# Reciprocal square roots of all norms: a chain of eleven VectorE instructions replaced by one GpSimd power instruction

## The chip, the cores and the metric

The kernel runs on one core of a Trainium2 chip. The core has TensorE for matrix products and transposes (PE in the profile, with its weight loads as PEld), VectorE (DVE), ScalarE (ACT), GpSimd (POOL) and SyncE, which issues most DMAs here (SP, its queue SPq). They run their own streams of instructions and meet through semaphores. The metric is the device time of one launch in microseconds, as a median of several runs.

## The reference, cut to what matters

One encoder layer is applied to two requests of 2048 tokens with 1024 features, in fp32. The normed input goes through one projection whose columns are split among two branches of attention. Both norm their queries and keys per head of 64 values:

```python
def rms_norm(x, g):
    y = xf * lax.rsqrt(jnp.mean(xf * xf, axis=-1, keepdims=True) + EPS)
    return (y * g).astype(x.dtype)

h = rms_norm(x, norm_w)
q_a, k_a, v_a, g_a, q_b, k_b, v_b, g_b = jnp.split(h @ w_in, IN_SPLITS, axis=-1)
q_a = partial_rope(rms_norm(q_a, q_norm_a), pos)    # 8 heads
k_a = partial_rope(rms_norm(k_a, k_norm_a), pos)    # 2 heads
o_a = windowed_gqa_sink(q_a, k_a, v_a, sink_a) * silu(g_a)
q_b, k_b = rms_norm(q_b, q_norm_b), rms_norm(k_b, k_norm_b)
o_b = neighbourhood_attn(q_b, k_b, v_b, rpb_b) * silu(g_b)
x = x + concat(o_a, o_b) @ w_out
x = x + (p @ w_ple) * sigmoid(x @ w_ple_gate)
```

Every `rsqrt` is one value per token (the norm of the input) or one per token and head (the norms of queries and keys).

## The kernel before, in words

Matrix products with full fp32 accuracy are made of three products of rounded halves: each operand is split into a rounded high part (written by ACT) and the rest (by DVE or POOL).

The program has three stages. In the **windowed stage**, 16 blocks of 128 tokens for each of two requests, about 57 to 770 us, each step of the loop projects one block (`proj_a`, L376) while PE also does the attention of the block before (`unit_a`, L492, two key-value heads, hence two units for each block). In the **neighbourhood stage**, about 772 to 1842 us, 64 steps do the same with `proj_b` (L559) and `unit_b` (L629): two halves of the heads, each over both requests. The **last stage** makes the output projection, the gate and the residual; it has no norms.

The input is not normed before it is projected. The projections are taken of the raw input and the factor is put in afterwards. So a block's norms need the mean square of the token (`square`, L283, by ACT from tiles `stn` that SP loads) and the mean squares of the projected heads, and then a reciprocal square root of each: `rsqrt` (L118). It is called

- in the key half of `proj_a` (L391): `vr` 8:11, three columns, two key heads and the token itself. Of its result `y` come the normed keys `kt` (L394, DVE), the values `vv` (L397, ACT) and the scale of the gate.
- in the query half of `proj_a` (L425): eight columns. Of them comes `q` (L427, DVE), which POOL then rotates (`rope`, L405 to L408).
- in `proj_b` (L584): eight columns, four key heads and four query heads. Of them come `kb` and `qg` (L588, DVE).
- in `stats_b` (L481): sixteen columns, twice in the program.

`rsqrt` takes a first guess from the bits of the number (L121, L123), then three Newton steps of three instructions each (L126, L127, L128), eleven DVE instructions on tiles of 128 partitions and 3, 8 or 16 columns.

The attention unit makes four score tiles (`sc`, `scb`: matmul L189), which DVE adds a mask or bias to and reduces to a maximum (L204); after the fourth, DVE negates the maxima (L215, L217), ACT takes four exponentials (L219) and PE transposes them (`pt`, `ptb`, L192). The score tiles and the transposes share three PSUM buffers, so that the fourth score tile is written where the first one was.

The order of PE is written out: `pinned` (L180) chains every matmul and transpose to the one before it, after a table of positions that mixes attention with the projections. The order of the other engines is the scheduler's, which takes each engine's instructions by when it estimates that they can run; it may move them past each other unless they depend on one another. Each engine then runs its own stream strictly in that order. At the end of each request, `regroup` (L469) writes the tokens' mean squares to memory and reads them back in another arrangement with 16 small loads on SP.

POOL makes the lower halves of the input (`xr`, L279), the rotations and the products with the gate (`g`, L229).

Of the kernel before, what the change touches and what calls it, by code (L numbers as in the profile page):

```python
# [11 lines left out]
F32 = mybir.dt.float32  # L12
F32R = mybir.dt.float32r
I32 = mybir.dt.int32
AF = mybir.ActivationFunctionType
ALU = mybir.AluOpType
# [4 lines left out]
NT = SEQ // 128  # L21
# [63 lines left out]
def emit(ctx, tc, io):  # L85
    nc = tc.nc
    dram = ctx.enter_context(tc.tile_pool(name="dram", bufs=1, space=bass.MemoryType.DRAM))
    cp = ctx.enter_context(tc.tile_pool(name="const", bufs=1))
# [11 lines left out]
    rs_b = cp.tile([128, 2 * NT], F32, tag="rs_b", name="rs_b")  # L100
    hr_b = cp.tile([128, 2 * NT], F32, tag="hr_b", name="hr_b")
    ep_b = cp.tile([128, 2 * NT], F32, tag="ep_b", name="ep_b")
    ms_b = cp.tile([128, 2 * NT], F32, tag="ms_b", name="ms_b")
    wk = cp.tile([128, 2], F32, tag="wk", name="wk")
    wkt = cp.tile([128, 4], F32, tag="wkt", name="wkt")
    nc.sync.dma_start(wkt, io["qk_norms"])
# [8 lines left out]
    ob_d = [dram.tile([4, 128, 4, 4, 128], F32, tag=f"ob_d{s}", name=f"ob_d{s}") for s in range(2)]  # L115
    ms_d = dram.tile([2 * SEQ], F32, tag="ms_d", name="ms_d")

    def rsqrt(pool, v, y, n, tag):  # L118
        i2 = pool.tile([128, n], I32, tag=tag + "i", name=tag + "i")
        a = pool.tile([128, n], F32, tag=tag + "a", name=tag + "a")  # L120
        nc.vector.tensor_scalar(out=i2, in0=v.bitcast(I32), scalar1=1, scalar2=None,  # L121
                                op0=ALU.logical_shift_right)
        nc.vector.tensor_scalar(out=y.bitcast(I32), in0=i2, scalar1=-1, scalar2=0x5F3759DF,  # L123
                                op0=ALU.mult, op1=ALU.add)
        for _ in range(3):
            nc.vector.scalar_tensor_tensor(out=a, in0=y, scalar=-0.5, in1=y, op0=ALU.mult, op1=ALU.mult)  # L126
            nc.vector.tensor_tensor(out=a, in0=a, in1=v, op=ALU.mult)  # L127
            nc.vector.scalar_tensor_tensor(out=y, in0=a, scalar=1.5, in1=y, op0=ALU.add, op1=ALU.mult)  # L128

    copies = []  # L130

# [113 lines left out]
    ap = ab_stack.enter_context(tc.tile_pool(name="ab", bufs=1))  # L245
# [98 lines left out]
    for i in range(4):  # L344
        nc.vector.tensor_tensor(out=tab[i // 2][:, i % 2], in0=cs[:, i % 2],
                                in1=rw[:, i].unsqueeze(1).broadcast_to([128, NT, 16]), op=ALU.mult)
# [29 lines left out]
    def proj_a(f):  # L376
# [8 lines left out]
                                op=ALU.add, axis=AX.X)  # L385
        vr = ap.tile([128, 11], F32, tag="vr", name="vr", bufs=2)
        y = ap.tile([128, 12], F32, tag="y", name="y", bufs=4)
        nc.vector.tensor_scalar(out=vr[:, 8:10], in0=ssq[:, 8:10], scalar1=1.0 / HD, scalar2=ee,
                                op0=ALU.mult, op1=ALU.add)
        nc.vector.tensor_scalar(out=vr[:, 10:11], in0=ms, scalar1=EPS, scalar2=None, op0=ALU.add)  # L390
        rsqrt(ap, vr[:, 8:11], y[:, 8:11], 3, "rqk")  # L391
        nc.vector.tensor_scalar_mul(y[:, 11:12], y[:, 10:11], 0.5)
        kt = ap.tile([128, 4, HD], F32, tag="kt", name="kt", bufs=2)
        nc.vector.tensor_tensor(out=kt[:, 0:2, :], in0=pk[:, 0:128].rearrange("p (h d) -> p h d", d=HD),  # L394
                                in1=y[:, 8:10].unsqueeze(2).broadcast_to([128, 2, HD]), op=ALU.mult)
# [3 lines left out]
                                       in1=vv[:, t, :, 0, :].bitcast(F32), op0=ALU.mult, op1=ALU.subtract)  # L399
# [12 lines left out]
        for i, c in enumerate(project(pq, xr, lambda k, b: w_q[k][:, b, :], 215)):  # L412
# [5 lines left out]
            if i == ka:  # L418
# [3 lines left out]
        nc.vector.tensor_reduce(out=ssq[:, 0:8], in_=sq.rearrange("p (h d) -> p h d", d=HD), op=ALU.add, axis=AX.X)  # L422
        nc.vector.tensor_scalar(out=vr[:, 0:8], in0=ssq[:, 0:8], scalar1=1.0 / HD, scalar2=ee,
                                op0=ALU.mult, op1=ALU.add)
        rsqrt(ap, vr[:, 0:8], y[:, 0:8], 8, "rqa")  # L425
        q = ap.tile([128, 8, HD], F32, tag="qg", name="q", bufs=6)
        nc.vector.tensor_tensor(out=q, in0=pq.rearrange("p (h d) -> p h d", d=HD),  # L427
                                in1=y[:, 0:8].unsqueeze(2).broadcast_to([128, 8, HD]), op=ALU.mult)
# [15 lines left out]
        if f == NT + 4:  # L444
            stats_b(0)
# [30 lines left out]
    def stats_b(s):  # L476
        c = slice(NT * s, NT * s + NT)
        tc.keep_in_program_order(nc.vector.tensor_scalar(out=ep_b[:, c], in0=ms_b[:, c], scalar1=EPS,
                                                         scalar2=EPS * EPS, op0=ALU.mult, op1=ALU.add))
        nc.vector.tensor_scalar(out=ms_b[:, c], in0=ms_b[:, c], scalar1=EPS, scalar2=None, op0=ALU.add)  # L480
        rsqrt(ap, ms_b[:, c], rs_b[:, c], NT, "rsb")  # L481
        nc.vector.tensor_scalar_mul(hr_b[:, c], rs_b[:, c], 0.5)

    def prep_a(f):
# [74 lines left out]
    def proj_b(f):  # L559
# [3 lines left out]
        if f == 2 * NT + 4:  # L563
            stats_b(1)
# [6 lines left out]
        for i, c in enumerate(project(pk, xr, lambda k, b: w_qk[k][:, b, :], 215)):  # L571
            at = i + 24 if f in last else i
            if at in HX:
# [6 lines left out]
        vr = ap.tile([128, 8], F32, tag="vr", name="vrb", bufs=2)  # L580
        y = ap.tile([128, 8], F32, tag="y", name="yb", bufs=4)
        nc.vector.tensor_scalar(out=vr, in0=ssq, scalar1=1.0 / HD, scalar2=ep_b[:, st:st + 1],
                                op0=ALU.mult, op1=ALU.add)
        rsqrt(ap, vr, y, 8, "rqb")  # L584
        qg = ap.tile([128, 2, 4, HD], F32, tag="qg", name="qg", bufs=6)
        kt = ap.tile([128, 4, HD], F32, tag="kt", name="kb", bufs=2)
        for dst, c in ((kt, 4), (qg[:, 0], 0)):
            nc.vector.tensor_tensor(out=dst, in0=pk[:, 64 * c:64 * c + 256].rearrange("p (h d) -> p h d", d=HD),  # L588
                                    in1=y[:, c:c + 4].unsqueeze(2).broadcast_to([128, 4, HD]), op=ALU.mult)
# [3 lines left out]
        for i, c in enumerate(project(pv, xr, lambda k, b: w_vg[k][:, b, :], 215)):  # L593
# [3 lines left out]
            if i == (KB if f not in last else 10):  # L597
                if f < 2 * NT + 2:
                    pending.append((kt, b, cb))
                else:  # L600
                    keys_b(kt, b, cb)
        v = ap.tile([128, 4, 2, HD], F32R, tag="sq", name="vb", bufs=2)
# [3 lines left out]
                                       in1=v[:, :, 0, :].bitcast(F32), op0=ALU.mult, op1=ALU.subtract)  # L606
# [179 lines left out]
    def filler(f):  # L786

        gen = proj_a(f) if f < 2 * NT else proj_b(f)
        for n, (cost, last_one) in enumerate(gen):
            if last_one:  # L790
                next(gen)
            elif n % 4 == 3:
                pump()
            yield cost
# [69 lines left out]
    with tc.tile_pool(name="c", bufs=1) as op:  # L864
# [179 lines left out]
        for m in range(7 * len(groups)):  # L1044
            n, i = divmod(m, 7)
# [104 lines left out]
```

## Time and profile before

| | |
|---|---|
| median of three runs | 2650.51 us (2650.36, 2650.51, 2655.77) |
| span of the profiled execution | 2651.7 us |
| PE busy | 2570.5 us, 97% |
| DVE busy | 1952.0 us, 74%, 5702 groups of instructions |
| ACT busy | 1500.2 us, 57% |
| POOL busy | 703.2 us, 27% |
| mean granted TensorE clock | 0.990 |

The profile is of one execution. Busy shares are over the whole program. In a timeline row the first number is the start and the second the duration, both in us, then engine, line, operation and tiles; in square brackets stands how long the engine had been idle before and what released it. In a row of groups the numbers after the bar are the busy time in us, the mean of one in ns, and the idle time of the engine just before.

### The profile page before, as it was taken

What the parts mean: (1) busy time and instruction counts of PE and PEld (TensorE: products, weight loads), DVE (VectorE), ACT (ScalarE), POOL (GpSimd) and SP (SyncE); (2) the same over time, 40 slices, a digit from 0 to 9 for tenths busy, and PEclk for the clock granted to TensorE, in tenths of its full rate; (3) what the DMA queues carried; (4) which work ended last, traced back from release to release, by engine and by line L of the source; (5) the groups of instructions that cost most, each with busy time, mean ns of one, the idle gap of its engine ahead of it and who ended that gap; (6) DMA issues with size and microseconds to landing.
All of it is one profiled execution on the core that took longest, in us unless ns stands there. A gap on an engine that the chain in (4) does not pass through costs nothing. (4 is left out here: it accounts for less than half of the span.)

```text
span 2651.7 us, 46657 instructions
## 1 busy us (share of the span) xinstructions
PE 2570.5 (97%) x16080; PEld 2270.6 (86%) x16080; DVE 1952.0 (74%) x5702; ACT 1500.2 (57%) x3519; POOL 703.2 (27%) x804
## 2 busy tenths in 40 slices
PE   7999999999989999999899999999989999999999
PEld 6888878888877888888788888888989999999999
DVE  6888878888887788788888888788665548555554
ACT  5776667676765566666676666666532214222322
POOL 3222222222222223223223222221123323223321
PEclk9999999999999999999999999999999999999999
DMA  6333322111233455555655554446675445223221
GB/s 208 101 100 102 108 74 77 58 55 52 55 98 117 150 170 171 181 177 160 221 167 165 185 170 153 148 152 205 184 235 195 158 158 194 79 97 107 80 76 48
DMA packets 230973, 357.48 MB, mean 135 GB/s; under 512 B 38321, under 2 KB 115761, under 8 KB 225585
## 3 DMA queue, kind: packets, MB, share of 16 engines
q1 hardware_dynamic: 230736, 354.51, 42.4%
q8 instruction: 127, 2.08, 0.3%
q14 instruction: 110, 0.89, 0.1%
HBM read 266.33 MB, written 105.92 MB: 140 GB/s over the span
## 5 line engine op out<-in xcount | busy, mean ns | idle before, releaser
L219 ACT ACTIVATE s<-s,nm 128x384 f32<-128x384 f32 (+4 forms) x512 | 306.3, 600 | 274.9 <-DVE nm L215 183.7
L189 PE MATMUL pvg<-wb,xr 128*128 128x512 f32 x1536 | 457.4, 405 | 0.0
L189 PE MATMUL pqk<-wa,xr 128*128 128x512 f32 x1536 | 436.6, 407 | 0.0
L279 POOL TENSOR_TENSOR xr<-stx,xr 128x512 fp32r<-128x512 f32 x192 | 246.9, 1296 | 396.1 <-ACT xr L278 369.2
L189 PEld LDWEIGHTS pqk<-wa,xr 128*128 128x128 f32 x1536 | 267.1, 189 | 36.8
L189 PEld LDWEIGHTS pvg<-wb,xr 128*128 128x128 f32 x1536 | 269.1, 190 | 31.8
L189 PE MATMUL pg<-wb,xr 128*128 128x512 f32 x768 | 231.9, 409 | 1.3 <-ACT wb L142 0.9
L189 PE MATMUL pq<-wa,xr 128*128 128x512 f32 x768 | 223.0, 404 | 3.5 <-DVE wa L143 2.3
L973 PE MATMUL acca<-opd,s 128*128 128x256 f32 x1344 | 169.6, 289 | 15.2 <-DVE r L992 13.6
L973 PEld LDWEIGHTS acca<-opd,s 128*128 128x128 f32 x1344 | 167.7, 197 | 15.8 <-DVE r L992 10.0
L189 PEld LDWEIGHTS pq<-wa,xr 128*128 128x128 f32 x768 | 141.6, 191 | 27.3 <-DVE wa L143 2.6
L204 DVE CUSTOM_DVE_ANT_0 s<-scb,bias 128x288 f32<-128x288 f32 (+3 forms) x256 | 141.9, 555 | 30.3 <-PE scb L189 26.4
L229 POOL TENSOR_TENSOR g<-qg,rd 128x256 f32<-128x256 f32 x64 | 39.2, 613 | 453.4 <-DVE rd L227 385.8
L668 DVE TENSOR_TENSOR p_t<-ptb,p_t 96x384 fp32r<-96x384 f32 (+3 forms) x256 | 149.6, 586 | 12.6 <-ACT p_t L667 9.1
L189 PEld LDWEIGHTS pob<-p_t,vw 128*128 128x128 f32 (+2 forms) x832 | 130.7, 190 | 32.4 <-ACT q1b L240 15.5
L189 PEld LDWEIGHTS pg<-wb,xr 128*128 128x128 f32 x768 | 137.2, 189 | 22.5 <-DVE wb L143 1.4
L667 ACT CAST p_t<-ptb 96x384 fp32r<-96x384 f32 (+3 forms) x256 | 129.8, 509 | 46.8 <-PE ptb L192 44.8
L556 DVE SCALAR_TENSOR_TENSOR ks_b<-pktb,wk,ks_b 64x128 fp32r<-64x128 f32 x256 | 115.2, 450 | 53.9 <-ACT ks_b L555 47.3
L189 PE MATMUL pob<-p_t,vw 128*128 128x256 f32 (+2 forms) x832 | 143.2, 285 | 5.4 <-ACT q1b L240 5.4
L189 PE MATMUL sc<-ks_a,q 128*128 128x384 f32 (+1 forms) x512 | 133.0, 351 | 13.2 <-DVE mx L204 6.4
L555 ACT ACTIVATE ks_b<-pktb,wk 64x128 fp32r<-64x128 f32 x256 | 124.9, 489 | 20.2 <-DVE ks_b L556 12.2
L204 DVE CUSTOM_DVE_ANT_0 s<-sc,mask 128x384 f32<-128x384 f32 (+1 forms) x256 | 136.0, 533 | 0.2
(197 smaller groups left out, 5826.3 us busy)
## 6 DMA issues: line engine op xcount, KB each, us to landing
stx<-x_b SPq DMA_DIRECT2D x128, 256.0 KB
vw<-v_d SPq DMA_DIRECT2D x112, 256.0 KB
stx<-x_a SPq DMA_DIRECT2D x64, 256.0 KB
stn<-x_n SPq DMA_DIRECT2D x64, 256.0 KB
v_d<-vb SPq DMA_DIRECT2D x64, 256.0 KB
x1r<-x_d SPq DMA_DIRECT2D x16, 1024.0 KB
y_t<-r SPq DMA_DIRECT2D x64, 256.0 KB
v_d<-vb SPq DMA_DIRECT2D x96, 128.0 KB
```

The costliest lines, as they stand in the source:

```text
L189: pinned(nc.tensor.matmul(out, lhsT, rhs, start=start, stop=stop))
L204: nc.vector.tensor_tensor_reduce(out=s[:, :n], in0=ps[:, :n], in1=bias, scale=1.0, scalar=-3.0e38, op0=ALU.add, op1=ALU.max, accum_out=sm[ ...
L219: nc.scalar.activation(ss[i][:, :n], ss[i][:, :n], AF.Exp, bias=nm[:, i:i + 1], accum_out=den[:, i:i + 1])
L229: nc.gpsimd.tensor_tensor(out=g2, in0=gs.rearrange("p (h d) -> p h d", h=4), in1=rd.unsqueeze(2).broadcast_to([128, 4, HD]), op=ALU.mult)
L279: nc.gpsimd.tensor_tensor(out=lo, in0=raw, in1=hi.bitcast(F32), op=ALU.subtract)
L555: nc.scalar.activation(hi, pkt[a:a + 64, i], AF.Copy, scale=wk[a:a + 64, 1:2])
L556: nc.vector.scalar_tensor_tensor(out=lo, in0=pkt[a:a + 64, i], scalar=wk[a:a + 64, 1:2], in1=hi.bitcast(F32), op0=ALU.mult, op1=ALU.subtract)
L667: nc.scalar.copy(p_t[:kc, :nch, 0], pf)
L668: nc.vector.tensor_tensor(out=p_t[:kc, :nch, 1], in0=pf, in1=p_t[:kc, :nch, 0].bitcast(F32), op=ALU.subtract)
L973: pinned(nc.tensor.matmul(ps[:, kk], w[k][:, a, c:c + 128], o[:, b, k], start=i in (0, 1, 4) and kk == 0 and k == 0 and j == 0, stop=k == ...
```

## The change

`rsqrt` loses its pool and tag arguments and becomes one instruction on POOL: the input to the power of -0.5, with the exponent from a constant tile `half_neg` that is set once at the start. The four calls change accordingly, and nothing else. From there on line numbers are 7 lower than before.

```diff
+    half_neg = cp.tile([128, NT], F32, tag="half_neg", name="half_neg")
+    nc.gpsimd.memset(half_neg, -0.5)
...
-    def rsqrt(pool, v, y, n, tag):
-        i2 = pool.tile([128, n], I32, tag=tag + "i", name=tag + "i")
-        a = pool.tile([128, n], F32, tag=tag + "a", name=tag + "a")
-        nc.vector.tensor_scalar(out=i2, in0=v.bitcast(I32), scalar1=1, scalar2=None,
-                                op0=ALU.logical_shift_right)
-        nc.vector.tensor_scalar(out=y.bitcast(I32), in0=i2, scalar1=-1, scalar2=0x5F3759DF,
-                                op0=ALU.mult, op1=ALU.add)
-        for _ in range(3):
-            nc.vector.scalar_tensor_tensor(out=a, in0=y, scalar=-0.5, in1=y, op0=ALU.mult, op1=ALU.mult)
-            nc.vector.tensor_tensor(out=a, in0=a, in1=v, op=ALU.mult)
-            nc.vector.scalar_tensor_tensor(out=y, in0=a, scalar=1.5, in1=y, op0=ALU.add, op1=ALU.mult)
+    def rsqrt(v, y, n):
+        nc.gpsimd.tensor_tensor(out=y, in0=v, in1=half_neg[:, :n], op=ALU.pow)
...
-        rsqrt(ap, vr[:, 8:11], y[:, 8:11], 3, "rqk")
+        rsqrt(vr[:, 8:11], y[:, 8:11], 3)
...
-        rsqrt(ap, vr[:, 0:8], y[:, 0:8], 8, "rqa")
+        rsqrt(vr[:, 0:8], y[:, 0:8], 8)
...
-        rsqrt(ap, ms_b[:, c], rs_b[:, c], NT, "rsb")
+        rsqrt(ms_b[:, c], rs_b[:, c], NT)
...
-        rsqrt(ap, vr, y, 8, "rqb")
+        rsqrt(vr, y, 8)
```

The order of PE's instructions is the same in both programs. The scheduler's order of the other engines differs in more places than the diff, because it places what follows by the new durations it assumes. Three places matter.

The first is DVE in the query half of a windowed block: `ssq` is the sum of squares per head, `vr` the mean with the constant, `pr` a part of the transposed exponentials, `s,mx` a score reduction (whose second row reads the maximum), `rqai` and `rqaa` tiles of the chain. Before:

```order
L422 TENSOR_REDUCE ssq<-sq 128x8
L518 TENSOR_TENSOR pr<-pt,pr 128x512
L423 TENSOR_SCALAR vr<-ssq,ee 128x8
L518 TENSOR_TENSOR pr<-pt,pr 128x512
L121 TENSOR_SCALAR rqai<-vr 128x8
L204 ISA s,mx<-sc,mask 128x384
L204 ISA mx 128x1
L123 TENSOR_SCALAR y<-rqai 128x8
L126 SCALAR_TENSOR_TENSOR rqaa<-y 128x8
L204 ISA s,mx<-sc,mask 128x384
L204 ISA mx 128x1
L127 TENSOR_TENSOR rqaa<-rqaa,vr 128x8
```

Now:

```order
L415 TENSOR_REDUCE ssq<-sq 128x8
L511 TENSOR_TENSOR pr<-pt,pr 128x512
L416 TENSOR_SCALAR vr<-ssq,ee 128x8
L511 TENSOR_TENSOR pr<-pt,pr 128x512
L420 TENSOR_TENSOR q<-pq,y 128x512
L197 ISA s,mx<-sc,mask 128x384
L197 ISA mx 128x1
```

The product `q`, which came after all four reductions and the whole chain, now stands ahead of the first reduction, and the power that it needs is on POOL.

The second is ACT and SP where a request ends. ACT in the key half before (`stn` is the squaring of the input, `s,den` an exponential):

```order
L383 ACTIVATE sq_4520<-pk 128x128
L292 ACTIVATE stn,ssq<-stn 128x512
L219 ACTIVATE s,den<-s,nm 128x384 x3
L397 ACTIVATE vv<-pk,y 128x2x64
L219 ACTIVATE s,den<-s,nm 128x384
L224 ACTIVATE es<-es 128x4
L537 COPY ot<-po 64x256
L292 ACTIVATE stn,ssq<-stn 128x512
```

And now:

```order
L376 ACTIVATE sq_4186<-pk 128x128
L285 ACTIVATE stn,ssq<-stn 128x512
L390 ACTIVATE vv<-pk,y 128x2x64
L285 ACTIVATE stn,ssq<-stn 128x512
L212 ACTIVATE s,den<-s,nm 128x384 x4
L217 ACTIVATE es<-es 128x4
```

The values `vv` and the second squaring moved ahead of all exponentials. SP at the same place before:

```order
L471 DMA ms_d<-ms_a 128x16x1
L474 DMA ms_b<-ms_d 128x1x1 x14
L261 DMA stn<-x_n 128x512
L540 DMA oa_d_86<-ot 128x2x128
L474 DMA ms_b<-ms_d 128x1x1 x2
L261 DMA stn<-x_n 128x512
```

And now:

```order
L464 DMA ms_d<-ms_a 128x16x1
L533 DMA oa_d_88<-ot 128x2x128
L467 DMA ms_b<-ms_d 128x1x1 x16
L533 DMA oa_d_88<-ot 128x2x128
L254 DMA stn<-x_n 128x512 x2
```

The loads of both `stn` tiles stand behind all sixteen regrouping loads, where the first one stood behind fourteen.

The third is DVE in a neighbourhood block (`vrb` and `yb` are there what `vr` and `y` are above, `nm` the negated maxima). Before:

```order
L204 ISA s,mx<-scb,bias 128x288
L204 ISA mx 128x1
L128 SCALAR_TENSOR_TENSOR yb<-rqba,yb 128x8
L215 TENSOR_SCALAR nm<-mx 128x4
L126 SCALAR_TENSOR_TENSOR rqba<-yb 128x8
L127 TENSOR_TENSOR rqba<-rqba,vrb 128x8
```

Now:

```order
L575 TENSOR_SCALAR vrb<-ssqb,ep_b 128x8
L197 ISA s,mx<-scb,bias 128x288
L197 ISA mx 128x1
L581 TENSOR_TENSOR kb<-pqk,yb 128x256
L197 ISA s,mx<-scb,bias 128x288
L197 ISA mx 128x1
L208 TENSOR_SCALAR nm<-mx 128x4
```

The product `kb` came after the negated maxima and the chain; it now stands ahead of the last reduction.

## The prediction

> **What bounds the kernel now.** The page's totals come first.
>
> ```profile
> span 2651.7 us, 46657 instructions
> PE 2570.5 (97%) x16080; PEld 2270.6 (86%) x16080; DVE 1952.0 (74%) x5702; ACT 1500.2 (57%) x3519; POOL 703.2 (27%) x804
> ```
>
> TensorE (PE) is busy for 97% of the span, so an instruction taken from VectorE (DVE) is worth something only where PE was waiting for it. PE's order is the same chained order of matmuls in both programs, so nothing can fill a hole. The next view is that of PE's waits, by what released them (total, times, longest, in us):
>
> ```profile
> PE sc L189 <- DVE mx L204: 6.4, 5, 2.5
> PE scb L189 <- DVE mx L204: 4.5, 2, 3.2
> PE pktb L192 <- DVE kb L588: 2.5, 3, 1.4
> PE scb L189 <- DVE vrb L582: 1.5, 1, 1.5
> PE pgtb L192 <- DVE rqba L127: 1.5, 1, 1.5
> PE pt L192 <- ACT s L219: 6.3, 4, 5.3
> ```
>
> The chain itself appears as a releaser once (rqba). The scb row shows more of it in the timeline around its 3.2 us wait, where weights are being split on DVE besides (columns: start, duration):
>
> ```profile
> 1293.94 2.91 POOL L279 TENSOR_TENSOR xr<-stx,xr 128x512 fp32r<-128x512 f32 x2 [10.01 <-ACT xr L278]
> 1294.41 1.25 DVE L127 TENSOR_TENSOR rqba<-rqba,vrb 128x8 f32<-128x8 f32 x1
> 1298.48 0.59 PE L189 MATMUL scb<-ks_b,q1b 128*128 128x512 f32 x1 [3.17 <-DVE mx L204]
> ```
>
> A multiply on 8 columns takes 1.25 us there, while POOL subtracts; DVE falls behind and the score reduction that PE awaits comes late. After such a hole PE runs at a lower granted clock, here 0.54 (columns: the length, five engines' busy times, then clock, DMA share and GB/s):
>
> ```profile
> 1298.40:1301.80 3.40, 3.32 (x10) 2.76 (x11) 3.40 (x10) 0.58 (x1) 0.00 (x0) 0.54 0.88 251
> ```
>
> **The change part by part.**
>
> *Removed: the DVE chains.* Most of them belong to the neighbourhood stage (32 and 32 more in the windowed stage, 2 for a whole request):
>
> ```profile
> L127 DVE TENSOR_TENSOR rqba<-rqba,vrb 128x8 f32<-128x8 f32 x192 | 35.7, 186 | 5.1
> L128 DVE SCALAR_TENSOR_TENSOR yb<-rqba,yb 128x8 f32<-128x8 f32 x192 | 35.7, 186 | 4.4
> L126 DVE SCALAR_TENSOR_TENSOR rqba<-yb 128x8 f32<-128x8 f32 x192 | 32.7, 170 | 5.4
> ```
>
> These three rows are 35.7+35.7+32.7 = 104 us of DVE time, over 1.6 us per block in its 64 blocks. Against a busy PE that is free time, not gain. The gain is bounded by the waits above that a chain can have made late: 4.5 (scb) + 2.5 (kb) + 1.5 (vrb) + 1.5 (rqba) = 10.0 us, and the half clock behind the largest, (1 - 0.54) x 3.40 = 1.6 us; together 11.6. Of the five sc waits I count none, since weight splits stand in them too. The lower bound is 0, if the splits alone make DVE late. I take 10, nearer the top, because each of these blocks has eleven chain operations in the way and collisions like the one shown: **-10**.
>
> *Added: one power instruction on POOL each.* No row of the trace has a power on any engine. The nearest rows are POOL's small two-input operations:
>
> ```profile
> L407 POOL TENSOR_TENSOR r<-kt,tab 128x16 f32<-128x16 f32 x32 | 7.1, 222 | 0.0
> L405 POOL TENSOR_TENSOR r<-kt,tab 128x32 f32<-128x32 f32 x32 | 8.6, 269 | 126.8 <-DVE kt L394 116.0 <-DVE tab L345 10.0 <-DVE den L225 0.7
> ```
>
> Lower bound: 0.22 us, as if a power were a multiply. Upper bound: eleven such operations, the work it replaces, 11 x 0.222 = 2.4 us. A power is a logarithm, a product and an exponential, so it is neither; I take the geometric middle, sqrt(0.22 x 2.4) = 0.73, say e = 0.75 us. The hand-over to POOL costs what kt's does:
>
> ```profile
> 665.20 0.28 DVE L394 TENSOR_TENSOR kt<-pk,y 128x128 f32<-128x128 f32 x1
> 665.56 0.25 POOL L405 TENSOR_TENSOR r<-kt,tab 128x32 f32<-128x32 f32 x1 [3.71 <-DVE kt L394]
> ```
>
> That is 665.56 - 665.48 = 0.08 us; with some 0.05 back, y is ready D = e + 0.13 = 0.88 us after the mean square (0.35 to 2.53 by the bounds). [...]
>
> *Moved: what stands behind the chain on DVE.* This decides. DVE runs in order. Before, a score reduction (L204) could slip in between two chain steps; now the one DVE instruction that needs y waits for POOL, and what is queued behind it waits too. In the windowed stage's query half the product q (L427) is placed ahead of all four score reductions:
>
> ```profile
> 646.65 0.22 DVE L423 TENSOR_SCALAR vr<-ssq,ee 128x8 f32<-128x8 f32 x1
> 646.78 0.68 DVE L518 TENSOR_TENSOR pr<-pt,pr 128x512 fp32r<-128x512 f32 x1
> 647.53 0.56 DVE L204 CUSTOM_DVE_ANT_0 s<-sc,mask 128x384 f32<-128x384 f32 x1
> 648.84 0.51 PE L189 MATMUL sc<-ks_a,q 128*128 128x384 f32 x2
> ...
> 515.36 0.54 DVE L204 CUSTOM_DVE_ANT_0 s<-sc,mask 128x384 f32<-128x384 f32 x1
> 515.96 0.62 PE L189 MATMUL sc<-ks_a,q 128*128 128x384 f32 x2 [0.77 <-DVE mx L204]
> ...
> L427 DVE TENSOR_TENSOR q<-pq,y 128x512 f32<-128x512 f32 x32 | 22.1, 691 | 1.1
> L204 DVE CUSTOM_DVE_ANT_0 s<-sc,mask 128x384 f32<-128x384 f32 x224 | 122.8, 550 | 0.2
> ```
>
> The mean square ends at 646.87, the pr subtraction at 647.46. The matmul of 648.84 is the fourth score tile; there are three score buffers, so it needs the first reduction done. With q ahead, that reduction ends at max(647.46, 646.87 + D) + 0.69 + 0.55, and PE starts 0.06 later (515.96 - 515.90 in a place where it waited for one). With D below 0.6 that is 648.76, in time for 648.84. Above, it is 648.17 + D, and PE loses D - 0.67 us. With D = 0.88 that is 0.21 us. The row x224 is eight reductions for each of 28 blocks with a full window: 28 x 0.21 = **+5.9**. By the bounds on e: 0, or 28 x (2.53 - 0.67) = 52 us. The four exponentials behind the reductions end later as well, but on ACT with room before their transposes.
>
> In the key half, the kt product stands between the second and third reduction, and ACT's order becomes square of x (L292), vv, square, then the four exponentials:
>
> ```profile
> 660.76 0.63 ACT L292 ACTIVATE stn<-stn 128x512 f32<-128x512 f32 x1
> 661.87 0.33 SPq L261 DMA_DIRECT2D stn<-x_n  x1
> 663.43 0.14 DVE L390 TENSOR_SCALAR vr<-ms_a 128x1 f32<-128x1 f32 x1
> 663.67 0.62 ACT L219 ACTIVATE s<-s,nm 128x384 f32<-128x384 f32 x1 [2.19 <-DVE nm L217]
> 667.68 0.60 PE L192 MATMUL pt<-ident,s 128*128 128x128 f32 x4
> ```
>
> The four exponentials took from 663.67 to 663.67 + 4 x 0.62 = 666.2 or a little later, and PE transposes the last of them by about 668.1, so they may slip by some 1.5 us. The kt product delays them by D and little more (0.88, hidden); vv and the second square, whose tile is only requested at 661.87, add about 1 us in place of D if that tile is there 2.6 us later. I count **0**; uncovered, each 0.1 us here would cost 28 x 0.1 = 2.8.
>
> In the neighbourhood stage kb (L588) moves between the third and fourth reduction:
>
> ```profile
> 1015.41 0.23 DVE L582 TENSOR_SCALAR vrb<-ssqb,ep_b 128x8 f32<-128x8 f32 x1
> 1016.62 0.53 DVE L204 CUSTOM_DVE_ANT_0 s<-scb,bias 128x360 f32<-128x360 f32 x1
> 1017.41 0.60 ACT L219 ACTIVATE s<-s,nm 128x360 f32<-128x360 f32 x1 [3.23 <-DVE nm L215]
> 1020.94 0.49 PE L192 MATMUL ptb<-ident,s 128*120 128x128 f32 x3
> ```
>
> y is there at 1015.64 + D = 1016.52, kb's 0.42 us then push the fourth reduction to about 1017.0, 0.4 late; ACT's exponentials start 0.4 late. PE first transposes a result of theirs at 1020.94, 2.9 us after the first was done (1017.41 + 0.60 = 1018.01). **0** up to D of about 3 us.
>
> *Moved: SP's loads at the end of a request.* There 16 small loads regroup the statistics:
>
> ```profile
> 340.94 9.16 SPq L474 DMA_DIRECT2D ms_b<-ms_d  x14
> 350.20 0.53 SPq L261 DMA_DIRECT2D stn<-x_n  x1
> 353.35 0.63 ACT L292 ACTIVATE stn<-stn 128x512 f32<-128x512 f32 x1 [11.16 <-DMA stn<-x_n]
> 354.73 1.67 PE L192 MATMUL pt<-ident,s 128*128 128x128 f32 x3 [5.35 <-ACT s L219]
> ```
>
> Fourteen took 9.16 us, 0.65 each, and held up the stn load that ACT waits for, 3.15 us from issue to use, and the exponentials behind it on ACT: one of PE's longest waits, 5.35 us. Now all 16 stand ahead of both stn loads, and both squares ahead of the exponentials: 2 x 0.65 + 0.63 = 1.9: **+2**. The range of this term is 0 to 4.
>
> *Sum*: -10 + 5.9 + 2 = -2, so 2651.7 - 2 = 2649.6 in the profiled execution's terms; it stood 1.2 us above the median of the runs, 2650.5, so the forecast is 2648.4, say **2648 us**.
>
> **The rivals.**
>
> *Cheap power* (e up to 0.5 us, close to a plain operation). Then q never stops PE: -10 + 2 = -8, so 2642 us. For it speaks that POOL's small operations are hardly dearer at 32 columns than at 16, that is, most of a small one is overhead; against, that a power is no single step.
>
> *Dear power: the wait for POOL replaces the chain, and the kernel gets slower.* The place is q ahead of the score reductions, the price 28 us for each us of D beyond 0.67. It outweighs the gain of 8 from D = 0.96, e = 0.83. At e = 1.5, D = 1.63: 28 x 0.96 = 27, some 4 more in the key half, -8: +23, 2673 us. At the upper bound 28 x 1.86 = 52, key half 28 x 1.2 = 34: +78, 2728. For it: DVE will sit idle where before it filled the time with reductions, and the chain it replaces is itself long. Against: nothing in the trace but the size of other POOL operations.
>
> *The tile in the key half*: the power is as forecast, but the second square waits for stn, and with it four exponentials, by 0.4 us in each block: +11, 2659 us. Each block's tile has about the time it needs, no more.
>
> *A power of several us*, which no row bounds. With e = 5, D = 5.1: 28 x 4.5 + 28 x 3.8 + 64 x 2.1 = 126 + 106 + 134 = +366, about 3015 us. [...]
>
> **How the numbers follow.** The forecast, e from 0.5 to 0.95 us and 2642 to 2653, has 0.36; the cheap power 0.20 (2638 to 2644); the dear one 0.29 (2653 to 2728); the late tile 0.06; several us 0.09. Single runs differ by about 0.2% at most, 5.3 us, which is taken as what a measurement can tell: below 2645.2 is faster, above 2655.8 slower. Faster takes the cheap power and about half the forecast, since its gain of 10 may be larger or its q stall smaller: 0.20 + 0.17 = 0.37. Slower takes the dear power but for its lowest part, the late tile's upper half and several us: 0.27 + 0.04 + 0.09 = 0.40, and 0.23 is left for no change. The range must leave no more than 2 in 10 out: several us and the dearest part of the dear power above, little below: 2636 to 2700. The forecast's own range is 2642 to 2653.
>
> **What would show it.** The mean of the power row on POOL settles e and with it most of the sum: under 0.5 the cheap rival, over 0.85 the dear one. In the query half PE's sc matmul should then wait some 0.2 us for mx, in most of 28 blocks; if no such group appears, this step is wrong. The waits scb on mx and pktb on kb should nearly vanish, the rqba row entirely; if they stay, the weight splits made them. The wait of pt on s should grow from 5.3 to about 7. The whole is wrong if PE waits for the power in the neighbourhood stage, or if the squares' tile shows as a releaser in ACT's waits.

## The result, and the profile after

The changed kernel takes 2744.26 us (median of four runs, 2742.69 to 2745.38) against 2651.34 us (2650.36 to 2655.77): 1.0348 times as long, 95% interval 1.0333 to 1.0363. The forecast was 2648 with a range up to 2700; the time lies above both, past the far end of the rival called dear power (2728) and far below that of a power of several us (3015).

The page's totals of the changed kernel:

```profile
span 2742.6 us, 45316 instructions
...
PE 2593.6 (95%) x16080; PEld 2268.0 (83%) x16080; DVE 1761.3 (64%) x4272; ACT 1491.6 (54%) x3519; POOL 896.4 (33%) x935
```

VectorE (DVE) did lose 1952.0 - 1761.3 = 191 us of work, and POOL gained 193 us. PE's work is the same 16080 matmuls. The span grew by 90.9 us: PE stood idle for 149.0 us in place of 81.2 (span less busy time), 67.8 us more, and its busy time grew by 23.1 us. Why the same matmuls are busy for longer is not shown; the mean granted clock, 0.989 after 0.990, is almost the same. PE's waits by releaser:

```profile
PE sc L182 <- DVE mx L197: 37.3, 28, 6.1
PE pktb L185 <- DVE otb L680: 18.5, 41, 1.5
PE sc L182 <- DVE pr L511: 14.3, 32, 4.1
PE pt L185 <- DVE ot L532: 14.2, 24, 2.7
...
PE pt L185 <- ACT s L212: 5.3, 5, 4.3
PE scb L182 <- DVE mx L197: 5.3, 3, 2.3
...
PE pktb L185 <- DVE kb L581: 1.2, 1, 1.2
```

sc on mx was 6.4 us in 5 waits and is 37.3 in 28; pktb on otb is new; sc on pr was 4.3 us in 25 waits, at most 0.4, and is 14.3 with one wait of 4.1; pt on ot stood so in the waits of the kernel before:

```profile
PE pt L192 <- DVE ot L539: 3.8, 3, 2.7
```

The power itself makes four of POOL's groups, one for each place where `rsqrt` is called, of three widths (busy, mean in ns, idle before):

```profile
L121 POOL TENSOR_TENSOR yb<-vrb,half_neg 128x8 f32<-128x8 f32 x64 | 106.2, 1659 | 189.2 <-DVE vrb L575 189.2
...
L121 POOL TENSOR_TENSOR y<-vr,half_neg 128x8 f32<-128x8 f32 x32 | 53.2, 1663 | 88.2 <-DVE vr L416 88.2
...
L121 POOL TENSOR_TENSOR y<-vr,half_neg 128x3 f32<-128x3 f32 x32 | 27.5, 860 | 20.6 <-DVE vr L381 14.9 <-DVE es L216 3.1
...
L121 POOL TENSOR_TENSOR rs_b<-ms_b,half_neg 128x16 f32<-128x16 f32 x2 | 5.8, 2905 | 0.1
```

Two of VectorE's groups stand idle for it the most, 84.4 + 38.3 us (another 16.5 and 5.9 us fall on what follows the powers of 3 and of 16 columns):

```profile
L581 DVE TENSOR_TENSOR kb<-pqk,yb 128x256 f32<-128x256 f32 x64 | 27.2, 424 | 84.4 <-POOL yb L121 84.4
...
L420 DVE TENSOR_TENSOR q<-pq,y 128x512 f32<-128x512 f32 x32 | 22.1, 691 | 38.3 <-POOL y L121 38.3
```

Since PE's order is the same in both programs, the two traces can be laid against each other matmul by matmul, and the growth of PE's lag can be put down to the place where it arises (worked out from the starts in the two traces, from PE's first matmul on; it holds waits and longer busy time alike; a jump is a step of over 0.15 us in either direction, and "pg to pt" is a pt that follows a pg):

| place | matmuls | lag gained, us |
|---|---|---|
| windowed stage, query half, fourth score tile (pg to sc) | 26 jumps | 32.3 |
| windowed stage, third transpose of the key half (pg to pt) | 23 jumps | 14.0 |
| windowed stage, one place behind `stats_b` (pq to sc) | 1 jump | 4.3 |
| windowed stage, all | | 53.2 |
| neighbourhood stage, transposes of the keys (pvg to pktb) | 50 jumps | 25.0 |
| neighbourhood stage, all | | 41.3 |
| program's end | | 90.3 |

One block of each of the three large places, and then the single one, from the timeline. The query half of a windowed block:

```profile
661.75 0.22 DVE L416 TENSOR_SCALAR vr<-ssq,ee 128x8 f32<-128x8 f32 x1
...
661.88 0.68 DVE L511 TENSOR_TENSOR pr<-pt,pr 128x512 fp32r<-128x512 f32 x1
...
662.05 1.65 POOL L121 TENSOR_TENSOR y<-vr,half_neg 128x8 f32<-128x8 f32 x1 [2.56 <-DVE vr L416]
...
663.73 0.69 DVE L420 TENSOR_TENSOR q<-pq,y 128x512 f32<-128x512 f32 x1 [1.17 <-POOL y L121]
664.34 0.55 DVE L197 CUSTOM_DVE_ANT_0 s<-sc,mask 128x384 f32<-128x384 f32 x1
...
664.95 0.62 PE L182 MATMUL sc<-ks_a,q 128*128 128x384 f32 x2 [1.18 <-DVE mx L197]
```

The mean square ends at 661.97, the hand-over takes 0.08, the power 1.65, the way back 0.03: D is 1.76 us. VectorE stands still for 1.17 us with three score tiles ready, and PE waits 1.18 us for the buffer of the first.

The key half of the same block:

```profile
649.51 2.55 SPq L254 DMA_DIRECT2D stn<-x_n  x2
...
651.79 0.86 POOL L121 TENSOR_TENSOR y<-vr,half_neg 128x3 f32<-128x3 f32 x1
...
654.39 0.17 DVE L210 SCALAR_TENSOR_TENSOR nm<-mx,snk 128x4 f32<-128x4 f32 x1
...
654.60 0.63 ACT L285 ACTIVATE stn<-stn 128x512 f32<-128x512 f32 x1 [1.09 <-DMA stn<-x_n]
...
655.23 0.60 ACT L212 ACTIVATE s<-s,nm 128x384 f32<-128x384 f32 x1
...
657.84 0.37 ACT L530 COPY ot<-po 64x256 f32<-64x256 f32 x1
...
658.69 0.36 ACT L530 COPY ot<-po 64x256 f32<-64x256 f32 x1 [0.48 <-DVE ot L531]
...
659.62 0.42 DVE L532 TENSOR_TENSOR ot<-pgt,ot 128x256 f32<-128x256 f32 x1
...
660.10 0.66 PE L185 MATMUL pt<-ident,s 128*128 128x128 f32 x4 [0.55 <-DVE ot L532]
```

The order of ACT that "The change" gives for the end of a request, both squarings ahead of the four exponentials, stands in nearly all windowed blocks. The negated maxima are there at 654.56, but ACT first squares a tile that it has waited 1.09 us for. The four exponentials start 0.67 us later than they could; behind them in ACT's queue are the two copies of the attention output, on which the product ot rests, and that product frees the buffer of the third transpose.

And a neighbourhood block:

```profile
1044.92 0.23 DVE L575 TENSOR_SCALAR vrb<-ssqb,ep_b 128x8 f32<-128x8 f32 x1
...
1045.22 1.65 POOL L121 TENSOR_TENSOR yb<-vrb,half_neg 128x8 f32<-128x8 f32 x1 [3.29 <-DVE vrb L575]
...
1046.90 0.42 DVE L581 TENSOR_TENSOR kb<-pqk,yb 128x256 f32<-128x256 f32 x1 [1.16 <-POOL yb L121]
...
1047.25 0.68 DVE L197 CUSTOM_DVE_ANT_0 s<-scb,bias 128x512 f32<-128x512 f32 x1
...
1048.17 0.72 ACT L212 ACTIVATE s<-s,nm 128x512 f32<-128x512 f32 x1 [4.95 <-DVE nm L208]
...
1051.13 0.58 ACT L679 COPY otb<-pob 64x512 f32<-64x512 f32 x1
...
1051.74 0.69 DVE L680 TENSOR_TENSOR otb<-pob,otb 64x512 f32<-64x512 f32 x1 [0.16 <-ACT otb L679]
...
1052.49 0.44 PE L185 MATMUL pktb<-ident,kb 128*128 128x128 f32 x2 [0.60 <-DVE otb L680]
```

The transpose of the keys, pktb, does not wait for its keys (kb is done at 1047.32) but for a PSUM buffer: pob holds it, and pob is read by a copy that ACT makes after the four exponentials. The exponentials are late because the fourth reduction stood behind kb, and kb behind the power.

The single place lies behind the power of 16 columns in `stats_b`, once in the windowed stage:

```profile
541.68 2.91 POOL L121 TENSOR_TENSOR rs_b<-ms_b,half_neg 128x16 f32<-128x16 f32 x1
...
544.62 1.23 DVE L475 TENSOR_SCALAR hr_b<-rs_b 128x16 f32<-128x16 f32 x1 [3.37 <-POOL rs_b L121]
545.77 1.27 DVE L511 TENSOR_TENSOR pr<-pt,pr 128x512 fp32r<-128x512 f32 x2
...
546.50 1.01 PE L182 MATMUL sc<-ks_a,q 128*128 128x384 f32 x2 [4.09 <-DVE pr L511]
```

VectorE waits 3.37 us in order for that power, two subtractions `pr` stand behind it, and PE waits 4.09 us for the first of them. With a multiplication in the power's place (run 1) PE does not wait there; in run 7, which moves all other users of a power, it still waits 2.6 us.

### The profile page after: what moved, and what is told of

Its sections match the earlier page's. It is cut to its first block, busy times and chain, and to the rows that moved or that the text cites. A ratio compares the mean times of both kernels' runs of the same rounds, so it can differ in the third digit from the quotient of the medians.

```text
span 2742.6 us, 45316 instructions
## 1 busy us (share of the span) xinstructions
PE 2593.6 (95%) x16080; PEld 2268.0 (83%) x16080; DVE 1761.3 (64%) x4272; ACT 1491.6 (54%) x3519; POOL 896.4 (33%) x935
## 5 line engine op out<-in xcount | busy, mean ns | idle before, releaser
L182 PE MATMUL sc<-ks_a,q 128*128 128x384 f32 (+1 forms) x512 | 134.8, 355 | 51.9 <-DVE mx L197 37.3
L966 PE MATMUL acca<-opd,s 128*128 128x256 f32 x1344 | 168.4, 287 | 14.9 <-DVE r L985 13.4
L121 POOL TENSOR_TENSOR yb<-vrb,half_neg 128x8 f32<-128x8 f32 x64 | 106.2, 1659 | 189.2 <-DVE vrb L575 189.2
L182 PEld LDWEIGHTS sc<-ks_a,q 128*128 128x128 f32 x512 | 88.2, 190 | 93.5 <-DVE mx L197 54.5
L932 POOL TENSOR_TENSOR opd<-sum,opd 128x1024 fp32r<-128x1024 f32 x28 | 69.7, 2488 | 231.5 <-ACT opd L918 231.5
L222 POOL TENSOR_TENSOR g<-gs,rd 128x256 f32<-128x256 f32 x64 | 39.3, 614 | 313.0 <-DVE rd L220 311.9
```

Source lines behind the costliest of these rows:

```text
L121: nc.gpsimd.tensor_tensor(out=y, in0=v, in1=half_neg[:, :n], op=ALU.pow)
L182: pinned(nc.tensor.matmul(out, lhsT, rhs, start=start, stop=stop))
L222: nc.gpsimd.tensor_tensor(out=g2, in0=gs.rearrange("p (h d) -> p h d", h=4), in1=rd.unsqueeze(2).broadcast_to([128, 4, HD]), op=ALU.mult)
L932: each(lambda x, y, z: eng.tensor_tensor(out=x, in0=y, in1=z, op=ALU.subtract), out, a, b)
L966: pinned(nc.tensor.matmul(ps[:, kk], w[k][:, a, c:c + 128], o[:, b, k], start=i in (0, 1, 4) and kk == 0 and k == 0 and j == 0, stop=k == ...
```

## The experiments

Twelve kernels were run, four at a time on one chip, each set beside its own runs of the kernel before (medians 2652.37, 2648.69 and 2650.40 us). "Lag" is PE's lag against the kernel before, as in the table above, for the windowed and the neighbourhood stage. Line numbers shift with each edit. The changed kernel was not run again in these sets; as the medians of the kernel before lie up to 3.7 us apart, differences from 2744.26 us are good to about 4 us.

### 1. A cheap instruction in the place of the power

```diff
-        nc.gpsimd.tensor_tensor(out=y, in0=v, in1=half_neg[:, :n], op=ALU.pow)
+        nc.gpsimd.tensor_tensor(out=y, in0=v, in1=half_neg[:, :n], op=ALU.mult)
```

> Each power is replaced by a multiplication on the same engine with the same tiles, so the norms are wrong, and every engine's order is that of the changed kernel word for word; only the duration of 131 POOL instructions changes. Theory 1 (VectorE waits in order for the power, and what is queued behind it reaches PE late): the multiplication takes 0.2 to 0.25 us at 8 columns, the wait of sc on mx in the query half (28.2 us in the windowed stage) and that of pktb on otb (18.5 us) nearly vanish, the wait of pt on ot shrinks by more than half, and the time is 2645 to 2665 us. Rival (the new order of the instructions is what costs, whatever the power takes): these waits stay within a third, and the time stays above 2700 us.

Measured: 2655.22 us, 1.0012 times before (1.0003 to 1.0022). The multiplication took 0.196 to 0.222 us at the three widths. Lag: 11.3 and -1.9 us. PE's waits:

```profile
PE pt L185 <- DVE ot L532: 13.6, 23, 2.7
...
PE sc L182 <- DVE mx L197: 7.4, 4, 4.2
```

So 89 of the 93 us are the power's duration, given this order. But one of the three large places did not move: pt on ot stayed at 13.6 us in 23 waits, which I had expected to shrink by more than half. That one is a matter of order, whatever the power takes; PE gains most of its 13 us back in other places.

### 2 to 4. The old chain back at one site each

```diff
-        rsqrt(vr[:, 0:8], y[:, 0:8], 8)
+        newton(ap, vr[:, 0:8], y[:, 0:8], 8, "rqa")
```

(`newton` is the old `rsqrt`; the next two runs do the same in the neighbourhood stage's call and in the key half's call.)

> The changed kernel with the old chain on VectorE back in the windowed stage's query half alone. Theory 1: the query half's wait of sc on mx (28 us, and some 4 us of slow clock and other waits) goes, the rest stays: 2744 - 32 = 2712 us, with the neighbourhood stage as long as in the changed kernel. Rival (POOL is too busy everywhere, or power instructions slow VectorE's own): the gain is spread over both stages, or below 15 us.

Measured: 2713.27 us. Lag 25.0 and 38.3 us: 28 of the 31 us came from the windowed stage.

> The changed kernel with the old chain back in the neighbourhood stage alone. Theory 1: the wait of pktb on otb (18.5 us) goes and the stage is about as long as in the kernel before (PE loses 41 us more there than before, of which some 4 lie at the seam with the windowed stage): 2744 - 37 = 2707 us, the windowed stage unchanged. Rival (wait of pktb has another cause, such as POOL's late xr): the wait stays.

Measured: 2705.33 us. Lag 51.6 and 3.5 us; the wait of pktb on otb is gone.

> The changed kernel with the old chain back in the windowed stage's key half alone. Theory 1: the wait of pt on ot (10.6 us in 22 places) goes, with the slower starts around it some 14 us: 2744 - 14 = 2730 us. Rival (that wait comes from the second squaring ahead of the exponentials on ACT, which waits for its tile, and not from the power): it stays if the squaring stays ahead, and the time is within 4 us of 2744.

Measured: 2724.32 us. Lag 29.4 and 42.0 us. The wait of pt on ot fell to 3.9 us, and the query half's jumps fell to 25 us besides, so the gain of 20 is more than the 14 expected. The scheduler's order around the key half changed with the chain (the second squaring stands behind the exponentials again), so this run alone doesn't tell the power from the order; run 1 does, and run 5 bears on it.

Two of the three estimates were within 2 us, the third 6 us off.

### 5. The second squaring behind the exponentials

A forced order, by the same kind of dependency that chains PE's instructions (`mark` remembers the last exponential):

```diff
-        nc.scalar.activation(xn, xn, AF.Square, accum_out=ssq[:, 10 + i:11 + i])
+        sqi = nc.scalar.activation(xn, xn, AF.Square, accum_out=ssq[:, 10 + i:11 + i])
+        if i == 1 and f >= 2:
+            after(sqi, "exp")
```

> The changed kernel with one order forced: the second squaring of the input comes after the last exponential on ACT (the scheduler then puts both there). Powers, and VectorE's order around them, stay. Theory 2 (in the key half the exponentials wait for the squaring's tile, not for the power; PE then waits for the buffer that the attention's output product frees): the wait of pt on ot falls from 14.2 to below 4 us, the exponentials of the key half start right after the negated maxima, and the time is 2744 - 13 = 2731 us. Rival (the power of three columns makes the exponentials late): the wait stays above 10 us and the time within 4 us of 2744.

Measured: 2745.76 us, no gain. Lag 56.3 and 38.0 us. By its letter the expectation failed and the rival's two numbers came out: the wait of pt on ot is 11.3 us, above 10, and the time is within 4 us of 2744. Where these waits lie says otherwise:

```profile
PE sc L190 <- DVE mx L205: 37.9, 29, 3.5
...
PE pt L193 <- DVE ot L542: 11.3, 5, 8.0
```

The 24 waits of pt on ot became 5, of which one of 8.0 us lies at the end of a request, and ACT's idle time for the tiles fell from 69.9 to 2.5 us. So the tile did hold up the third transposes, in part at least, and the time did not follow. Against the changed kernel PE gained 7.9 of the 14 us at the third transposes and lost 5.2 in the query half, where each of the waits grew from 1.18 to about 1.37 us: PE came earlier to a place where VectorE was not. Another 9.4 us net went at the ends of the requests (waits of 8.0 and 6.1 us), where the new order put the regrouping loads ahead of weights and input that PE needed. A wait was taken away from in front of another one.

### 6. q behind the maxima, power in place

```diff
-        nc.vector.tensor_tensor(out=q, in0=pq.rearrange("p (h d) -> p h d", d=HD),
-                                in1=y[:, 0:8].unsqueeze(2).broadcast_to([128, 8, HD]), op=ALU.mult)
-        rope(q, 8, 0)
...
+            if i == 10:
+                after(nc.vector.tensor_tensor(out=q, in0=pq.rearrange("p (h d) -> p h d", d=HD),
+                                              in1=y[:, 0:8].unsqueeze(2).broadcast_to([128, 8, HD]), op=ALU.mult), "nm")
+                rope(q, 8, 0)
```

> The changed kernel with the power in place, but q, which needs it in the windowed stage's query half, forced behind the negated maxima on VectorE, as it was before the change. Theory 1 (the place of q in VectorE's order makes the power's time a stall): the wait of sc on mx falls from 37.3 to below 10 us and the time to 2744 - 32 = 2712 us, as with the chain put back there. Rival (POOL's power slows the reductions or the transposes' inputs whatever the order): less than half of that is gained.

Measured: 2691.07 us. Lag 2.3 and 39.4 us: the windowed stage was back to its old length with every power on POOL. The gain is 53 instead of 32 us, because the jumps at the third transposes went too (-13.8 against the changed kernel) while the wait of sc on pr grew from 14.3 to 20.8 us. I had not expected the first. ACT still has both squarings ahead of the exponentials in this run, but its idle time for their tiles fell from 69.9 to 17.2 us; SP's order changed along with the edit. That fits the late tile as the cause at the third transposes, without separating it from q's move.

### 7 and 8. All users of the power late, and the control

Run 7 also defers kt, vv, kb and qg behind the negated maxima, and puts the second squaring behind the output copies. Run 8 forces the same places with the old chains on VectorE. The part of the edit for the neighbourhood stage:

```diff
+            if i == 9:
+                for dst, cc in ((kt, 4), (qg[:, 0], 0)):
+                    after(nc.vector.tensor_tensor(out=dst, in0=pk[:, 64 * cc:64 * cc + 256].rearrange("p (h d) -> p h d", d=HD),
+                                                  in1=y[:, cc:cc + 4].unsqueeze(2).broadcast_to([128, 4, HD]), op=ALU.mult), "nm")
```

> All powers stay on POOL; all that need them (kt, vv, q, kb, qg) are forced behind the negated maxima on VectorE, and the second squaring behind the output copies on ACT. Theories 1 and 2 together: none of the three waits of the changed kernel is left, 2744 - 32 - 37 - 13 = 2662 us, and less as in the multiplication's run, where the seams between the stages came out better too: 2640 to 2655 us. Theory 3 (the chains on VectorE cost nothing but the largest waits, which belong to the splitting of weights): not measurably faster than before, 2646 to 2655 us. If the chains cost PE 10 us, as the prediction had it, 2640 us.

Measured: 2646.54 us, 0.9991 times before (0.9982 to 1.0000): the whole loss of 93 us is gone with the same 130 powers on POOL, and no difference from before can be told. Run 2's rival, that powers on POOL slow VectorE whatever the order, is not needed for any of the 93 us. Lag 1.2 and -5.7 us.

```profile
PE pt L193 <- DVE ot L547: 14.5, 5, 9.4
...
PE sc L190 <- DVE mx L205: 4.9, 3, 2.5
...
PE pt L193 <- ACT s L220: 3.7, 1, 3.7
```

> The forced order of the run before it, with the old chains on VectorE in place of the powers: the control for it. If the order alone is what helps or hurts, both take the same time. Theories 1 and 2: about the time of the kernel before, 2645 to 2660 us, since the order is nearly the same as there; the difference to the run before it is the worth of taking the chains off VectorE.

Measured: 2673.23 us, 1.0092 (1.0078 to 1.0105). Lag 27.7 and -2.6 us. That is 13 us above the range expected, which had taken this order to be nearly that of the kernel before. Nor is it quite run 7's: what was left free to the scheduler on VectorE and ACT came out otherwise in places, so the control is not clean. With these places forced the power is 27 us better than the chain, nearly all in the windowed stage (waits of pt on ot 11.8 us in 28 places, of sc on pr 13.4 us, of which one of 8.3). So "off VectorE" has a value that depends on the order as well.

### 9. kb alone behind the maxima

> The changed kernel with kb and qg alone (neighbourhood stage) forced behind the negated maxima on VectorE; powers stay. Theory 1: the fourth reduction no longer waits for the power, the wait of pktb on otb (18.5 us) goes, and the stage is about as long as before: 2744 - 37 = 2707 us, as with the chain put back there (2705). Rival (the duration of the power makes kb itself late for its own transpose): the wait moves to pktb on kb, and less than half is gained.

Measured: 2701.80 us. Lag 51.9 and -0.5 us; the wait of pktb on otb is gone, and none on kb took its place. The neighbourhood stage's 41 us hung on the place of two instructions behind the power.

### 10. The output copy on VectorE

```diff
-                nc.scalar.copy(ot[a:a + 64], pq[z:z + 64])
+                nc.vector.tensor_copy(out=ot[a:a + 64], in_=pq[z:z + 64])
```

> The changed kernel with the copy of the attention output of the neighbourhood stage (otb from pob) on VectorE instead of ACT, where it was queued behind the four exponentials; kb keeps its place ahead of the fourth reduction. Theory 3 (the late exponentials reach PE through this copy, which frees the PSUM buffer that pktb takes, and not through their own transposes): the wait of pktb on otb vanishes though the exponentials are as late as in the changed kernel, and PE's transposes of the exponentials do not begin to wait: 2744 - 30 = 2714 us. Rival (the exponentials themselves are too late): the time lost moves to ptb on s, 2735 to 2745 us.

Measured: 2781.48 us, slower by another 37 us where 30 less were expected. The part on the waits held:

```profile
PE pob L182 <- ACT q1b L233: 53.0, 52, 2.5
...
PE pktb L185 <- DVE kb L581: 1.2, 1, 1.2
...
PE ptb L185 <- ACT s L212: 0.2, 1, 0.2
```

The wait of pktb on otb vanished (26.2 us less at these matmuls) and the transposes of the exponentials did not begin to wait, which is what the buffer's theory says. But 48.8 us came back at pob, which then waited for ACT's casts of the queries to free the other buffer of the same pair. Why those casts came later was not followed further.

### 11 and 12. The regrouping loads spread out

The waits of 9.4 and 3.7 us in run 7 lie where the 16 small loads stand on SP, all in a row at the end of the first request and mixed with loads of weights at the second. Here two of them are issued behind each later load of the input, in run 11 on top of run 7, in run 12 on the kernel before:

```diff
+        for g in regs[:2]:
+            tc.keep_in_program_order(g())
+            regs.pop(0)
```

> The run with all power users behind the maxima, and besides the 32 small loads that regroup the statistics issued two at a time behind later loads of the input instead of 16 in a row. Its waits of pt for 9.4 and 3.7 us at the two ends of a request stood behind these loads: if they are the cause, both waits fall below 3 us, 2646.5 - 8 = 2638 us, with the lower clock behind such holes some 2 us less still. If weight tiles or the input were late anyway, 2644 to 2650 us.

Measured: 2636.15 us, 0.9945 times before (0.9933 to 0.9958). Lag -10.4 and -3.0 us. The wait of 3.7 us is gone; that of 9.4 fell to 4.2 us and not below 3: there ACT waits 4.8 us for a weight tile first.

> The kernel before with the same spreading of the 32 small loads, chains on VectorE: its wait of 5.35 us at the first end of a request should fall below 2 us; 2650 - 4 to - 6 = 2645 us. The difference to the run before this one is what the power on POOL is worth where nothing waits for it: theory 4 of the prediction (chains cost 10 us) 7 us or more, else under 5.

Measured: 2645.23 us, 0.9978 (0.9968 to 0.9987). Lag -6.0 and 0.7 us, of which 5.5 at the pt that had waited 5.35 us and no longer waits.

Run 11 beats both kernels, by 14 us the kernel before. In both pairs (11 and 7, 12 and before) the orders of PE, VectorE, ACT and POOL are the same, so the spreading alone is worth 10.4 us in the forced order and 5.2 us in the kernel before: the two changes don't simply add up. With the loads spread, the powers on POOL with their users out of the way are 9.1 us better than the chains; with the loads in a row they were 2.1 us better, at the limit of what can be told. The order was forced along with the powers, so these are the worth of both together.

## Why the prediction was wrong, point by point

**What bounds the kernel: right.** PE's waits decided everything; 191 us taken from VectorE bought nothing in the changed kernel.

**Gain from the chains, -10: near in size once nothing waits for the power, but not all where I put it.** By run 12's expectation 7 us or more between runs 11 and 12 spoke for a gain of 10, and 9.1 were measured. Of the lag between the two, 3.7 us lie in the neighbourhood stage, where I had all 10, and 4.4 in the windowed stage, where I had none. In run 7 the neighbourhood stage's scb, pktb and pgtb matmuls came 3.5 + 2.1 + 1.4 = 7.0 us earlier than before, the stage as a whole 5.7. With the cheap multiplication the stage gained 1.9. In the changed kernel the sum of scb on mx did not shrink (4.5 before, 5.3 after). Yet the chain did make the wait of 3.17 us shown in the prediction: at the same matmul it is 0.15 us with the power in run 7 and 3.27 with the chain in the same forced places in run 8. In the changed kernel, where kb waits for the power ahead of the last reduction, it is 1.52.

**The power's price, e = 0.75 us: mis-sized.** It measured 1.66 us at 8 columns (means of 1.659 and 1.663), inside the bounds of 0.22 and 2.4. I took the geometric middle of ends a factor of eleven apart for want of a nearer row; the upper bound, "the work it replaces", was the better guide. How a power is made inside, no run shows: the logarithm, the product and the exponential were my arithmetic for it and stand in no row of a trace. Nor does a run show the 5 us of the last rival: of the powers of the changed kernel the longest took 2.91 us, at 16 columns.

**q ahead of the reductions, 28 x (D - 0.67): right in mechanism and near in size.** With the measured D of 1.76 it gives 28 x 1.09 = 30.5 us; 32.3 were measured in 26 jumps, with a wait of 1.18 in the block shown. Its price of +5.9 was too small because e was. With e at 0.22 (run 1) the stall was gone (VectorE stood idle 0.3 us in all for q's input, where the power made it 38.3), as the formula has it below D = 0.67.

**Key half, 0: wrong, and for a reason that stood among the rivals.** "The tile in the key half" had 0.06 of the chances and a price of 11; 14.0 us were measured. It was no alternative to a dear power, as I had it, but comes on top, since it hangs on ACT's order: it was there at 13.3 us with a cheap multiplication (run 1). The sign that I had set for it came up: ACT's idle time for the squares' tiles went from 23.3 us in 21 places to 69.9 in 50. I had checked how late the exponentials may be for their own transposes, and not the two copies queued behind them on ACT.

**Neighbourhood stage, 0 up to D of about 3: the step that failed.** 41 us were measured, 25 of them in front of pktb. I took the exponentials' first use by PE as the deadline (2.9 us away). The nearer one was behind them in the same queue, the copy of pob, and it stood in the trace of before:

```profile
1019.86 0.58 ACT L686 COPY otb<-pob 64x512 f32<-64x512 f32 x1
...
1020.47 0.69 DVE L687 TENSOR_TENSOR otb<-pob,otb 64x512 f32<-64x512 f32 x1 [0.16 <-ACT otb L686]
...
1021.74 0.38 PE L192 MATMUL pktb<-ident,kb 128*128 128x128 f32 x2
```

The buffer was free at 1021.16 and pktb started at 1021.74: less the 0.06 us from the one to the other (1052.43 to 1052.49 in the block shown above), a slack of some 0.52 us, not 2.9. By the same block, the power's D of 1.8 us makes y ready at 1015.64 + 1.8 = 1017.44 and kb done at 1017.86, so the fourth reduction starts there instead of at 1016.62, 1.2 us late; less 0.52 that is a stall of 0.7; of the 41 waits measured 25 are 0.45 to 0.62 us and 15 shorter. By the same sum the delay of 0.4 at my e of 0.75 would have stayed within that slack, so the two errors needed each other. The places downstream of this (pob, the later pktb, the seam with the windowed stage) make up the rest of the 41 us; all of it went when kb and qg moved (run 9).

**The power of `stats_b`: at nothing without a reason.** I counted its two chains among those removed and gave its power no place in the sum. The first of the two cost 4.3 us.

**Regrouping, +2: not seen.** The wait of pt on the exponentials there went from 5.3 to 4.3 us. That these loads cost PE time at all was right (runs 11 and 12).

**The sum.** With e measured and all else as it stood, my terms give -10 + 30.5 + 2 = +22.5, about 2673 us, which lies within the stated range: the dear power alone does not explain the miss. Of the missing 70 us, 51 are the neighbourhood stage's (41 lost where my terms had 10 gained), 14 the key half's transposes and 4 the power of `stats_b`; what is left is about 1 us.

## What to carry to other kernels

Moving a result to another engine turns its time from work into latency (here 191 us less work on VectorE, and 84.4 + 38.3 us of its time idle ahead of kb and q); what it costs is set by where the first user of that result stands in a queue that is worked off in order (q ahead of the reductions: 32.3 us lost; q behind the maxima, run 6: the windowed stage 2.3 us from its old length), so look up what is queued behind that user, and behind what that in turn delays, on every engine, down to the buffers they free (pktb on otb: 18.5 us). The deadline of a delayed group is the earliest among its own users and those of everything queued behind it (0.52 us at pktb, where the exponentials' own transposes left 2.9). Where the result is slow to come, put its users behind the work that is ready (with the same powers 93 us were lost, and all of them won back). An operation that no row shows has a wide range of prices; here the work it replaces (2.4 us) was nearer to the 1.66 measured than the cheapest instruction of its engine (0.22), so a term that turns into loss with the price is to be worked out at the dear end too.

## What the runs showed of the hardware

A power on POOL is priced by its columns, unlike the multiplication: 0.86, 1.66 and 2.91 us at 3, 8 and 16 columns (a fit to these three: about 0.39 us and 0.157 us for each column of 128 values), against 0.196, 0.22 and 0.222 us (run 1). At 8 columns it takes as long as nine or ten VectorE operations of the old chain (0.16 to 0.19 us each), so the eleven that it replaces were 1.8 to 2.0 us of VectorE added up, or 1.5 us of its busy time (191 us over 130 chains), since neighbouring operations overlap (in the prediction's rows `vr` runs to 646.87, and the next one starts at 646.78).
